# Gate and up of a SwiGLU layer: Strassen's seven products in every second step, sums on VectorE

## The chip, the core and the metric

The kernel runs on one core of one Trainium2 chip. The metric is the device time of one execution in microseconds. A core has TensorE for matrix products, VectorE, ScalarE and GpSimd for the rest, an SBUF of 128 partitions and a PSUM of eight banks (128 x 512 float32 each). Every engine has a queue of its own instructions and goes through it in order; SP here only issues transfers.

## The reference

One decoder layer for 256 tokens of width 2048 in float32. Two token mixers (an attention with compressed, selected and windowed keys, and a gated delta rule) work on the same normalised input, are merged by gates, projected and added to x. What the change touches is the feed-forward part behind them, with D_FF = 5632:

```python
x = x + mix @ w_out
h2 = _rms_norm(x, ffn_norm)
x = x + (jax.nn.silu(h2 @ w_gate) * (h2 @ w_up)) @ w_down
```

All weights and activations are float32.

## The kernel before

The 256 tokens are two tiles of 128 (t = 0, 1), the width of 2048 is 16 k-tiles of 128, and D_FF is 11 blocks of 512 columns. A weight tile of two k-tiles by 512 columns is loaded as `raw` [128, 2, 512] (512 KB) by SP, in `load_pair` (L99). Products are made in a reduced float32 format; to keep the precision, each operand is split into a high part (the number in that format) and a low part (the rest), and a product takes three matmuls: high by high, high by low, low by high. ScalarE copies raw to `whi` (L107), VectorE subtracts to `wlo` (L108):

```python
hi = stream.tile([P, 2, 512], F32R, tag="whi", name=nm("whi"), bufs=3)
lo = stream.tile([P, 2, 512], F32R, tag="wlo", name=nm("wlo"), bufs=3)
nc.scalar.activation(hi[:, :, :width], raw[:, :, :width], AF.Copy)
nc.vector.tensor_tensor(
    lo[:, :, :width], raw[:, :, :width], hi[:, :, :width].bitcast(F32), ALU.subtract
```

`raw` has four buffers, `whi` and `wlo` three each, all in the pool `stream`. A tile of raw is free again when its two readers, the copy and the subtraction, are done.

`chunk_tok` (L113) multiplies the activations (stationary, one k-tile by 128 tokens at a time) with 512 columns of weights, for both tiles of tokens, into two PSUM banks. For each pair of k-tiles it issues 12 matmuls of 128 x 128 by 128 x 512 (L122 to L124: two k-tiles, two token tiles, three each). For gate and up it runs over 8 pairs, so 96 matmuls, and a block of gate and up has 192.

A block of gate and up is one `chunk_tok` for w_gate, whose `evac_gate` (L1051) writes Silu(PSUM x rs2) on ScalarE into `sg` (rs2 is the reciprocal norm of each token), and one for w_up, whose `evac_up` (L1058) multiplies with PSUM and rs2 on VectorE; then `transpose_hilo` (L179) turns the result in eight transposes on TensorE (L183) and splits it (L176 on ScalarE, L177 on VectorE) into the tiles `act` in SBUF, the stationary operand of w_down. Eleven blocks follow each other, then four chunks of 512 columns of w_down over all 44 k-tiles, whose result is added to x2 (L1078) and written out.

The program is written in the order of the loops, and a scheduler that comes with the language puts the instructions of each engine into their final order by its own model of their times. So an engine's queue need not follow the code line by line; the excerpts of the order below show what came out.

Of the kernel before, what the change touches and what calls it, by code (L numbers as in the profile page):

```python
# [1115 lines left out]
```

## Time and profile before

| | us |
|---|---|
| median of three runs | 1974.73 (1974.52 to 1977.64) |
| span of the profiled execution | 1971.1 |
| TensorE busy in it | 1946.4 |
| VectorE busy | 1155.0 |
| ScalarE busy | 928.4 |
| from the transposes of one gate/up block to those of the next | 44.41 |

The time of a run is the device's, the span that of the profiled execution from its first to its last instruction. Busy times are summed over an engine's instructions; a busy TensorE counts matmuls that lie in its pipeline, so 1946.4 of 1971.1 says that it hardly ever stood, not that it ran at its peak. The last row is read from the chain that ended last.

### The profile page before, as it was taken

What the parts mean: (1) busy time and instruction counts of PE and PEld (TensorE: products, weight loads), DVE (VectorE), ACT (ScalarE), POOL (GpSimd) and SP (SyncE); (2) the same over time, 40 slices, a digit from 0 to 9 for tenths busy, and PEclk for the clock granted to TensorE, in tenths of its full rate; (3) what the DMA queues carried; (4) which work ended last, traced back from release to release, by engine and by line L of the source; (5) the groups of instructions that cost most, each with busy time, mean ns of one, the idle gap of its engine ahead of it and who ended that gap; (6) DMA issues with size and microseconds to landing.
All of it is one profiled execution on the core that took longest, in us unless ns stands there. A gap on an engine that the chain in (4) does not pass through costs nothing.

```text
span 1971.1 us, 27260 instructions
## 1 busy us (share of the span) xinstructions
PE 1946.4 (99%) x10485; PEld 1651.0 (84%) x10485; DVE 1155.0 (59%) x1715; ACT 928.4 (47%) x1377; POOL 54.1 (3%) x97
## 2 busy tenths in 40 slices
PE   8999999999999999999999999999999999999999
PEld 6878877876998998999987788888888888888887
DVE  5555766655468587687774665554455444544443
ACT  5434555555454554654543544444444444443333
POOL 0001000001000000100100000000000000000000
PEclk9999999999999999999999999999999999999999
DMA  8566545546767566566574965666666666656663
GB/s 231 170 183 193 161 129 162 170 149 200 217 173 203 169 178 198 158 193 166 153 200 157 333 201 183 191 192 183 191 191 186 191 191 191 191 185 201 201 202 130
DMA packets 207605, 367.04 MB, mean 186 GB/s; under 512 B 25473, under 2 KB 34546, under 8 KB 207090
## 3 DMA queue, kind: packets, MB, share of 16 engines
q1 hardware_dynamic: 207442, 365.28, 62.1%
q8 instruction: 82, 1.34, 0.3%
q14 instruction: 49, 0.40, 0.1%
q10 hardware_dynamic: 32, 0.01, 0.0%
HBM read 355.76 MB, written 9.45 MB: 185 GB/s over the span
## 4 chain that ended last, share of the span: by engine, by line
PE 96%; DMA 2%; DVE 1%; ACT 0%; SPq 0%; issue 0%; POOL 0%; ACTq 0%; POOLq 0%; DVEq 0%
PE mm L123 25%; PE mm L124 24%; PE mm L122 24%; PE mm L141 4%; PE mm L143 4%; PE mm L142 4%; PE sd L183 1%; PE sd L668 1%; PE sd L448 1%; PE sd L561 1%; DMA Q<-grow_d 1%; PE sd L748 1%; DMA raw<-in_w_branch_b_dram 1%; PE sd L567 1%; PE sd L568 0%; PE sd L267 0%
## 5 line engine op out<-in xcount | busy, mean ns | idle before, releaser
L108 DVE TENSOR_TENSOR wlo<-raw,whi 128x1024 fp32r<-128x1024 f32 x632 | 773.7, 1225 | 658.5 <-ACT whi L107 656.1
L107 ACT ACTIVATE whi<-raw 128x1024 fp32r<-128x1024 f32 x632 | 669.7, 1060 | 804.5 <-PE mm L124 674.4
L123 PE MATMUL mm<-wlo,hT_hi 128*128 128x512 f32 x704 | 276.7, 393 | 0.0
L124 PE MATMUL mm<-whi,hT_lo 128*128 128x512 f32 x704 | 276.5, 393 | 0.0
L124 PE MATMUL mm<-whi,h2T_lo 128*128 128x512 f32 x704 | 274.0, 389 | 0.0
L123 PE MATMUL mm<-wlo,h2T_hi 128*128 128x512 f32 x704 | 273.9, 389 | 0.0
L122 PE MATMUL mm<-whi,hT_hi 128*128 128x512 f32 x704 | 260.2, 393 | 0.0
L122 PE MATMUL mm<-whi,h2T_hi 128*128 128x512 f32 x704 | 249.9, 390 | 0.0
L143 PE MATMUL mm<-hT_hi,wlo 128*128 128x256 f32 x768 | 218.4, 285 | 0.0
L141 PE MATMUL mm<-hT_hi,whi 128*128 128x256 f32 x768 | 218.4, 285 | 0.0
L142 PE MATMUL mm<-hT_lo,whi 128*128 128x256 f32 x768 | 218.3, 284 | 0.0
L124 PEld LDWEIGHTS mm<-whi,hT_lo 128*128 128x128 f32 x704 | 132.3, 188 | 27.7 <-issue 1.1
L123 PEld LDWEIGHTS mm<-wlo,hT_hi 128*128 128x128 f32 x704 | 132.3, 188 | 27.5 <-issue 1.1
L124 PEld LDWEIGHTS mm<-whi,h2T_lo 128*128 128x128 f32 x704 | 132.2, 188 | 27.5
L122 PEld LDWEIGHTS mm<-whi,h2T_hi 128*128 128x128 f32 x704 | 132.2, 188 | 27.1
L123 PEld LDWEIGHTS mm<-wlo,h2T_hi 128*128 128x128 f32 x704 | 132.2, 188 | 27.0
L122 PEld LDWEIGHTS mm<-whi,hT_hi 128*128 128x128 f32 x704 | 132.1, 188 | 26.3 <-issue 0.2
L141 PEld LDWEIGHTS mm<-hT_hi,whi 128*128 128x128 f32 x768 | 147.2, 192 | 0.6
L142 PEld LDWEIGHTS mm<-hT_lo,whi 128*128 128x128 f32 x768 | 147.2, 192 | 0.2
L143 PEld LDWEIGHTS mm<-hT_hi,wlo 128*128 128x128 f32 x768 | 146.9, 192 | 0.4
L123 PE MATMUL mm<-wlo,act 128*128 128x512 f32 x352 | 138.5, 393 | 0.0
L124 PE MATMUL mm<-whi,act 128*128 128x512 f32 x352 | 138.4, 393 | 0.0
...
## 6 DMA issues: line engine op xcount, KB each, us to landing
raw<-in_w_in_dram SPq DMA_DIRECT2D x272, 512.0 KB, 3.7
raw<-in_w_gate_dram SPq DMA_DIRECT2D x88, 512.0 KB, 4.4
raw<-in_w_up_dram SPq DMA_DIRECT2D x88, 512.0 KB, 3.7
raw<-in_w_down_dram SPq DMA_DIRECT2D x88, 512.0 KB, 4.7
raw<-in_w_branch_a_dram SPq DMA_DIRECT2D x32, 512.0 KB, 4.7
raw<-in_w_branch_b_dram SPq DMA_DIRECT2D x32, 512.0 KB, 4.9
raw<-in_w_out_dram SPq DMA_DIRECT2D x32, 512.0 KB, 4.7
...
```

Source lines behind the costliest of these rows:

```text
L107: nc.scalar.activation(hi[:, :, :width], raw[:, :, :width], AF.Copy)
L108: nc.vector.tensor_tensor(lo[:, :, :width], raw[:, :, :width], hi[:, :, :width].bitcast(F32), ALU.subtract)
L122: nc.tensor.matmul(o, lhsT=sh, rhs=hi[:, j, :width], start=kt == 0, stop=False)
L123: nc.tensor.matmul(o, lhsT=sh, rhs=lo[:, j, :width], start=False, stop=False)
L124: nc.tensor.matmul(o, lhsT=sl, rhs=hi[:, j, :width], start=False, stop=kt == kts - 1)
L141: nc.tensor.matmul(o, lhsT=hi[:, j, ws], rhs=xh[:, kt, :], start=first, stop=False, skip_group_check=True)
L142: nc.tensor.matmul(o, lhsT=hi[:, j, ws], rhs=xl[:, kt, :], start=False, stop=False, skip_group_check=True)
L143: nc.tensor.matmul(o, lhsT=lo[:, j, ws], rhs=xh[:, kt, :], start=False, stop=last, skip_group_check=True)
L183: nc.tensor.transpose(pt[:, i * P : (i + 1) * P], s4, ident)
L448: nc.tensor.matmul(pc[:60, :P], lhsT=kp[:, l0 + l, :], rhs=wc[:, l, :], start=l0 + l == 0, stop=l0 + l == 31)
L561: nc.tensor.transpose(pt[:n, r * P : (r + 1) * P], pb[:, r, c0 : c0 + n], ident)
L567: nc.tensor.matmul(po, lhsT=wh, rhs=ph[:n], start=i == 0, stop=False)
```

## The change

Eleven blocks become one as before (block 0) and ten new ones. Block 0 writes its result to DRAM (`act_d`) in place of transposing it. Beside its matmuls, a side task `factors` makes the stationary operands of the new blocks: it multiplies the normalised activations by the token's norm (a row of norms, `rsrow`, comes from one matmul with ones), takes the sums that Strassen's scheme needs, and splits them, 13 tiles `Fh` and `Fl` for each of four groups of k-tiles.

In the new blocks gate and up are multiplied together. Step j (0 to 7) takes k-tiles j and 8 + j of w_gate and of w_up, so four tiles of 128 x 512, in two raw tiles of 512 KB (`raw_step`). The two k-tiles, the two token tiles, and gate and up make a product of 2 x 2 blocks by 2 x 2 blocks. An odd step (`eight_step`) takes its eight products, 24 matmuls. An even step (`seven_step`) takes seven, 21 matmuls, of which four have sums of weight tiles as their moving operand. These sums are made on VectorE, four of 128 x 512 for a step (tiles `ta` and `tb`), and then split into `thi` on ScalarE and `tlo` on VectorE like the weights; of the tile of up only one half is split. The products go to seven PSUM banks `M`, in which the eight products of the odd steps are accumulated too, so that gate and up come out by the same few sums. These are taken once at the end of a block: one copy, two Silu on ScalarE and nine operations on VectorE (`strassen_block`). Blocks 1 and 2 transpose and split their result into SBUF at once (`act_r`). Blocks 3 to 10 write theirs to `act_d`. The first chunk of w_down begins with blocks 1 and 2; beside it a side task `act_in` brings the other nine blocks back from DRAM, transposes and splits them.

The order on TensorE, in its matmuls until w_out has ended, is as before; the program has 9951 matmuls in place of 10070.

The order on VectorE shows what stands there in the place of the weights' subtractions. Before, in the middle of gate/up, VectorE has the subtractions of one raw tile after another, and at a block's end two multiplications and the two splits:

```order
L108 TENSOR_TENSOR wlo_2421_14740<-raw_2419_14737,whi_2420_14739 128x1024
L108 TENSOR_TENSOR wlo_2424_14758<-raw_2422_14755,whi_2423_14757 128x1024
L108 TENSOR_TENSOR wlo_2431_14794<-raw_2429_14791,whi_2430_14793 128x1024
L108 TENSOR_TENSOR wlo_2434_14812<-raw_2432_14809,whi_2433_14811 128x1024
L1058 SCALAR_TENSOR_TENSOR sg_2397_14623<-mm_2399_14627,rs2_11664,sg_2397_14623 128x512
L1058 SCALAR_TENSOR_TENSOR sg_2398_14625<-mm_2400_14628,rs2_11664,sg_2398_14625 128x512
L108 TENSOR_TENSOR wlo_2437_14830<-raw_2435_14827,whi_2436_14829 128x1024
```

Now, in block 7 at its third step (step 2: raw_2455 is its gate tile, raw_2456 its up tile; raw_2467 and raw_2468 are those of step 3, raw_2473 is the gate tile of step 4; y_2429 belongs to the end of block 6), VectorE has these twelve rows:

```order
L1157 TENSOR_TENSOR ta_2457_14343<-raw_2455_14339,raw_2456_14341 128x512
L1158 TENSOR_TENSOR ta_2457_14343<-raw_2456_14341 128x512
L182 TENSOR_TENSOR wlo_2460_14350<-raw_2455_14339,whi_2459_14349 128x1024
L1208 TENSOR_TENSOR y_2429_14234<-y_2429_14234,v_2427_14232 128x512
L1160 TENSOR_TENSOR tb_2458_14346<-ta_2457_14343,raw_2456_14341 128x512
L182 TENSOR_TENSOR tlo_2462_14354<-ta_2457_14343,thi_2461_14353 128x1024
L182 TENSOR_TENSOR wlo_2466_14362<-raw_2456_14341,whi_2465_14361 128x512
L1161 TENSOR_TENSOR tb_2458_14346<-tb_2458_14346,raw_2455_14339 128x512
L182 TENSOR_TENSOR wlo_2470_14391<-raw_2467_14386,whi_2469_14390 128x1024
L182 TENSOR_TENSOR wlo_2472_14395<-raw_2468_14388,whi_2471_14394 128x1024
L182 TENSOR_TENSOR tlo_2464_14358<-tb_2458_14346,thi_2463_14357 128x1024
L182 TENSOR_TENSOR wlo_2478_14433<-raw_2473_14422,whi_2477_14432 128x1024
```

The sums stand between the subtractions, and the last row is the first for the next step of seven. Beyond this excerpt the sums ta of step 4 follow.

In block 2 the rows stand in another order. Here raw_2033 is the up tile of step 1, raw_2038 and raw_2039 are the gate and up tiles of step 2, raw_2050 and raw_2051 those of step 3, raw_2056 and raw_2057 those of step 4:

```order
L182 TENSOR_TENSOR wlo_2037_12515<-raw_2033_12508,whi_2036_12514 128x1024
L182 TENSOR_TENSOR wlo_2043_12553<-raw_2038_12542,whi_2042_12552 128x1024
L182 TENSOR_TENSOR wlo_2049_12565<-raw_2039_12544,whi_2048_12564 128x512
L182 TENSOR_TENSOR wlo_2053_12594<-raw_2050_12589,whi_2052_12593 128x1024
L1157 TENSOR_TENSOR ta_2058_12629<-raw_2056_12625,raw_2057_12627 128x512
L1158 TENSOR_TENSOR ta_2058_12629<-raw_2057_12627 128x512
L1160 TENSOR_TENSOR tb_2059_12632<-ta_2058_12629,raw_2057_12627 128x512
L182 TENSOR_TENSOR wlo_2055_12598<-raw_2051_12591,whi_2054_12597 128x1024
```

Here the last subtractions that read the tiles of step 2 stand two and three rows ahead of the first sum of step 4.

The core of the diff; what is left out are comments, the moving of pools, and the closing of those that are no longer used:

```diff
-    def chunk_tok(w, c0, width, kts, stat, evac):
-        ps = [psm.tile([P, 512], F32, tag="mm", name=nm("mm")) for _ in range(NT)]
-        for k0 in range(0, kts, 2):
+    def chunk_tok(w, c0, width, kts, stat, evac, order=None):
+        ps = [mps() for _ in range(NT)]
+        pairs = order or list(range(0, kts, 2))
+        for n, k0 in enumerate(pairs):
             hi, lo = load_pair(w, k0, c0, width)
             for j in range(2):
-                kt = k0 + j
+                first, last = n + j == 0, j == 1 and n == len(pairs) - 1
                 for t in range(NT):
-                    sh, sl = stat(kt, t)
+                    sh, sl = stat(k0 + j, t)
                     o = ps[t][:, :width]
-                    nc.tensor.matmul(o, lhsT=sh, rhs=hi[:, j, :width], start=kt == 0, stop=False)
+                    nc.tensor.matmul(o, lhsT=sh, rhs=hi[:, j, :width], start=first, stop=False)
                     nc.tensor.matmul(o, lhsT=sh, rhs=lo[:, j, :width], start=False, stop=False)
-                    nc.tensor.matmul(o, lhsT=sl, rhs=hi[:, j, :width], start=False, stop=kt == kts - 1)
+                    nc.tensor.matmul(o, lhsT=sl, rhs=hi[:, j, :width], start=False, stop=last)
             yield
...
+    A12, A11, A22, S1, S3, S2, S4 = range(7)
+    B12, B11, B22, B21, B3, B5 = range(7, 13)
+    Fh = [fac.tile([P, 13, P], F32R, name=f"Fh{g}") for g in range(4)]
+    Fl = [fac.tile([P, 13, P], F32R, name=f"Fl{g}") for g in range(4)]
+    def tmp(n):
+        return fin.tile([P, 512], F32, tag="tmp", name=nm(n), bufs=6)
+    def factors():
+        dg = tmp("dg")
+        for t in range(NT):
+            nc.vector.tensor_scalar_mul(dg[:, t * P : (t + 1) * P], ident, rs2[:, t : t + 1])
+        one = tmp("one")
+        nc.vector.memset(one[:, :P], 1.0)
+        pr = sps()
+        nc.tensor.matmul(pr[:, :S], lhsT=one[:, :P], rhs=dg[:, :S], start=True, stop=True)
+        nc.scalar.activation(rsrow, pr[:, :S], AF.Copy)
+        yield
+        hv = h2T_hi.bitcast(F32).rearrange("p (h k) s -> p h k s", h=2)
+        lv = h2T_lo.bitcast(F32).rearrange("p (h k) s -> p h k s", h=2)
+        for g in range(4):
+            js = slice(2 * g, 2 * g + 2)
+            q = ft.tile([P, 4, 2, P], F32, tag="q", name=nm("q"))
+            for t in range(NT):
+                ts = slice(t * P, (t + 1) * P)
+                qt = q[:, 2 * t : 2 * t + 2]
+                nc.vector.tensor_tensor(qt, hv[:, :, js, ts], lv[:, :, js, ts], ALU.add)
+                qf = qt.rearrange("p h k c -> p (h k) c")
+                nc.vector.tensor_tensor(qf, qf, rsrow[:, ts].unsqueeze(1).to_broadcast([P, 4, P]), ALU.mult)
+            yield
+            sm = ft.tile([P, 6, P], F32, tag="sm", name=nm("sm"))
+            e, o = q[:, :, 0, :], q[:, :, 1, :]
+            nc.vector.tensor_tensor(sm[:, 0], e[:, 3], e[:, 2], ALU.subtract)
+            nc.vector.tensor_tensor(sm[:, 1], e[:, 1], e[:, 3], ALU.subtract)
+            nc.vector.tensor_tensor(sm[:, 2], e[:, 1], sm[:, 0], ALU.subtract)
+            nc.vector.tensor_tensor(sm[:, 3], e[:, 0], sm[:, 2], ALU.subtract)
+            nc.vector.tensor_tensor(sm[:, 4], o[:, 1], o[:, 3], ALU.subtract)
+            nc.vector.tensor_tensor(sm[:, 5], o[:, 0], o[:, 2], ALU.subtract)
+            hilo(Fh[g][:, 0:3], Fl[g][:, 0:3], e[:, 0:3])
+            hilo(Fh[g][:, 3:7], Fl[g][:, 3:7], sm[:, 0:4])
+            hilo(Fh[g][:, 7:11], Fl[g][:, 7:11], o)
+            hilo(Fh[g][:, 11:13], Fl[g][:, 11:13], sm[:, 4:6])
+            yield
...
-    def evac_gate(c):
-        def f(t, ps):
-            sg[t] = fin.tile([P, 512], F32, tag="tmp", name=nm("sg"), bufs=6)
-            nc.scalar.activation(sg[t], ps, AF.Silu, scale=rs2[:, t : t + 1])
-
-        return f
-
-    def evac_up(c):
-        def f(t, ps):
-            a = sg[t]
-            nc.vector.scalar_tensor_tensor(a, ps, rs2[:, t : t + 1], a, ALU.mult, ALU.mult)
-            k0 = 4 * c
-            transpose_hilo(
-                [a[:, i * P : (i + 1) * P] for i in range(4)], act[0][k0 // 16], act[1][k0 // 16], k0 % 16, t
-            )
-
-        return f
-
-    for c in range(DFF // 512):
-        run(chunk_tok(w_gate, c * 512, 512, KD, stat_h2, evac_gate(c)))
-        run(chunk_tok(w_up, c * 512, 512, KD, stat_h2, evac_up(c)))
+    def evac_gate(t, ps):
+        sg[t] = tmp("sg")
+        nc.scalar.activation(sg[t], ps, AF.Silu, scale=rs2[:, t : t + 1])
+    def evac_up(t, ps):
+        nc.vector.scalar_tensor_tensor(sg[t], ps, rs2[:, t : t + 1], sg[t], ALU.mult, ALU.mult)
+        nc.sync.dma_start(act_d[0, t], sg[t])
+    side.append(factors())
+    run(chunk_tok(w_gate, 0, 512, KD, stat_h2, evac_gate))
+    run(chunk_tok(w_up, 0, 512, KD, stat_h2, evac_up))
+    drain()
...
+    def split(src, n, pool, tag, bufs):
+        hi = pool.tile([P, 2, 512], F32R, tag=tag[0], name=nm(tag[0]), bufs=bufs)
+        lo = pool.tile([P, 2, 512], F32R, tag=tag[1], name=nm(tag[1]), bufs=bufs)
+        hilo(hi[:, :n], lo[:, :n], src[:, :n])
+        return hi, lo
+    def raw_step(j, c):
+        raw = []
+        for n in ("g", "u"):
+            raw.append(stream.tile([P, 2, 512], F32, tag="raw", name=nm("raw")))
+            nc.sync.dma_start(raw[-1], halves[n][j][:, :, c * 512 : (c + 1) * 512])
+        return raw
+    def products(terms, M, j, first, last):
+        seen, final = set(), {m: i for i, (m, *_) in enumerate(terms)}
+        g = j // 2
+        for i, (m, f, hi, lo) in enumerate(terms):
+            nc.tensor.matmul(M[m], lhsT=Fh[g][:, f], rhs=hi, start=first and m not in seen, stop=False)
+            nc.tensor.matmul(M[m], lhsT=Fh[g][:, f], rhs=lo, start=False, stop=False)
+            nc.tensor.matmul(M[m], lhsT=Fl[g][:, f], rhs=hi, start=False, stop=m in last and final[m] == i)
+            seen.add(m)
+    def seven_step(j, c, M):
+        g, u = raw_step(j, c)
+        b21, b11, b22, b12 = g[:, 0], g[:, 1], u[:, 0], u[:, 1]
+        ta = sw.tile([P, 2, 512], F32, tag="T", name=nm("ta"), bufs=3)
+        nc.vector.tensor_tensor(ta[:, 0], b11, b12, ALU.add)
+        nc.vector.tensor_tensor(ta[:, 1], b22, b12, ALU.add)
+        tb = sw.tile([P, 2, 512], F32, tag="T", name=nm("tb"), bufs=3)
+        nc.vector.tensor_tensor(tb[:, 0], ta[:, 0], b22, ALU.add)
+        nc.vector.tensor_tensor(tb[:, 1], tb[:, 0], b21, ALU.add)
+        gh, gl = split(g, 2, stream, ("whi", "wlo"), 3)
+        ah, al = split(ta, 2, sw, ("thi", "tlo"), 4)
+        bh, bl = split(tb, 2, sw, ("thi", "tlo"), 4)
+        uh, ul = split(u, 1, stream, ("whi", "wlo"), 3)
+        terms = [
+            (1, A11, gh[:, 1], gl[:, 1]),
+            (2, A12, gh[:, 0], gl[:, 0]),
+            (7, S3, ah[:, 1], al[:, 1]),
+            (5, S1, ah[:, 0], al[:, 0]),
+            (6, S2, bh[:, 0], bl[:, 0]),
+            (4, A22, bh[:, 1], bl[:, 1]),
+            (3, S4, uh[:, 0], ul[:, 0]),
+        ]
+        if j == 0:
+            terms = [terms[i] for i in (0, 4, 2, 3, 6, 5, 1)]
+        products(terms, M, j, j == 0, (1, 6, 7) if j == 6 else ())
+    def eight_step(j, c, M):
+        g, u = raw_step(j, c)
+        gh, gl = split(g, 2, stream, ("whi", "wlo"), 3)
+        uh, ul = split(u, 2, stream, ("whi", "wlo"), 3)
+        u0, u1, g0, g1 = ((h[:, i], l[:, i]) for h, l in ((uh, ul), (gh, gl)) for i in range(2))
+        if j == 7:
+            terms = [(5, B22, *u0), (5, B21, *u1), (3, B5, *u0), (3, B3, *u1)]
+            terms += [(4, B22, *g0), (4, B21, *g1), (2, B12, *g0), (2, B11, *g1)]
+        else:
+            terms = [(4, B22, *g0), (4, B21, *g1), (2, B12, *g0), (2, B11, *g1)]
+            terms += [(5, B22, *u0), (5, B21, *u1), (3, B5, *u0), (3, B3, *u1)]
+        products(terms, M, j, False, (2, 3, 4, 5) if j == 7 else ())
+    def strassen_block(c):
+        M = {m: mps() for m in (1, 6, 7, 5)}
+        M.update({m: sps() for m in (3, 4, 2)})
+        for j in range(8):
+            (eight_step if j % 2 else seven_step)(j, c, M)
+        m1, v, x, y = tmp("m1"), tmp("v"), tmp("x"), tmp("y")
+        nc.scalar.activation(m1, M[1], AF.Copy)
+        nc.vector.tensor_tensor(v, M[6], m1, ALU.subtract)
+        nc.vector.tensor_tensor(y, v, M[7], ALU.subtract)
+        nc.vector.tensor_tensor(x, M[5], v, ALU.add)
+        nc.vector.tensor_tensor(v, M[5], y, ALU.add)
+        nc.vector.tensor_tensor(x, M[3], x, ALU.add)
+        nc.vector.tensor_tensor(y, M[4], y, ALU.subtract)
+        nc.scalar.activation(y, y, AF.Silu)
+        nc.vector.tensor_tensor(m1, M[2], m1, ALU.add)
+        nc.scalar.activation(m1, m1, AF.Silu)
+        nc.vector.tensor_tensor(y, y, v, ALU.mult)
+        nc.vector.tensor_tensor(x, m1, x, ALU.mult)
+        for t, a in enumerate((x, y)):
+            if c > 2:
+                nc.sync.dma_start(act_d[c, t], a)
+                continue
+            pt = sps()
+            for i in range(4):
+                nc.tensor.transpose(pt[:, i * P : (i + 1) * P], a[:, i * P : (i + 1) * P], ident)
+            ks, ts = slice(4 * c - 4, 4 * c), slice(t * P, (t + 1) * P)
+            hilo(act_r[0][:, ks, ts], act_r[1][:, ks, ts], pt.rearrange("p (k c) -> p k c", k=4))
+    for c in range(1, NB):
+        strassen_block(c)
...
+    rest = [0] + list(range(3, NB))
+    act_l = {c: [actp.tile([P, 4, S], F32R, name=f"act{q}_{c}") for q in range(2)] for c in rest}
+    def act_in():
+        for c in rest:
+            for t in range(NT):
+                a = tmp("a")
+                nc.sync.dma_start(a, act_d[c, t])
+                transpose_hilo([a[:, i * P : (i + 1) * P] for i in range(4)], act_l[c][0], act_l[c][1], 0, t)
+            yield
 
     def stat_act(kt, t):
...
+    order = [4 * c + k for c in [1, 2] + rest for k in (0, 2)]
+    side.append(act_in())
     for c in range(4):
-        run(chunk_tok(w_down, c * 512, 512, KF, stat_act, evac_down(c)))
+        run(chunk_tok(w_down, c * 512, 512, KF, stat_act, evac_down(c), order), 1)
```

## Rows read from the trace of the kernel before

**Rows 1.** The page's first part: busy time, share of the span, instructions.

```profile
span 1971.1 us, 27260 instructions
PE 1946.4 (99%) x10485; PEld 1651.0 (84%) x10485; DVE 1155.0 (59%) x1715; ACT 928.4 (47%) x1377; POOL 54.1 (3%) x97
```

**Rows 2.** The page's fourth part: the chain that ended last, by engine.

```profile
PE 96%; DMA 2%; DVE 1%; ACT 0%; SPq 0%; issue 0%; POOL 0%; ACTq 0%; POOLq 0%; DVEq 0%
```

**Rows 3.** Busy time by engine in one gate/up block (windows; columns first).

```profile
core 0: us, PE busy (x) PEld busy (x) DVE busy (x) ACT busy (x) POOL busy (x), PEclk, DMA share, GB/s
1282.40:1326.80 44.40, 44.40 (x203) 36.87 (x201) 22.21 (x21) 19.32 (x20) 0.00 (x0) 1.00 0.65 191
```

**Rows 4.** The chain in order of time, gate/up: start, us, what.

```profile
1282.42 0.87 PE sd L183 x8
1326.83 0.87 PE sd L183 x8
```

**Rows 5.** TensorE's timeline in gate/up: start, us, line, operation.

```profile
1374.73 0.39 PE L122 MATMUL mm<-whi,h2T_hi 128*128 128x512 f32 x1
1374.96 0.39 PE L123 MATMUL mm<-wlo,h2T_hi 128*128 128x512 f32 x1
1375.19 0.39 PE L124 MATMUL mm<-whi,h2T_lo 128*128 128x512 f32 x1
```

**Rows 6.** VectorE by line and shape: count | busy, mean ns | idle before, releaser.

```profile
L108 DVE TENSOR_TENSOR wlo<-raw,whi 128x1024 fp32r<-128x1024 f32 x632 | 773.7, 1225 | 658.5 <-ACT whi L107 656.1
...
L708 DVE TENSOR_SCALAR Q<-Q,gcum 128x128 f32<-128x128 f32 x32 | 7.1, 281 | 6.7 <-DMA Q<-grow_d 6.7
...
L989 DVE TENSOR_TENSOR ba<-ba,ga 128x512 f32<-128x512 f32 x8 | 5.5, 682 | 2.1 <-DMA ba<-brA_d 2.1
...
L1078 DVE TENSOR_TENSOR x<-mm,x 128x512 f32<-128x512 f32 x8 | 5.2, 684 | 5.4 <-PE mm L124 5.4
```

**Rows 7.** VectorE's timeline at two places in gate/up.

```profile
1498.18 1.23 DVE L108 TENSOR_TENSOR wlo<-raw,whi 128x1024 fp32r<-128x1024 f32 x1 [1.49 <-ACT whi L107]
1499.33 1.40 DVE L1058 SCALAR_TENSOR_TENSOR sg<-mm,rs,sg 128x512 f32<-128x512 f32 x2
...
1372.37 1.29 DVE L177 TENSOR_TENSOR act<-sd,act 128x512 fp32r<-128x512 f32 x2 [0.80 <-ACT act L176]
```

**Rows 8.** ScalarE by line and shape, the split of a weight tile.

```profile
L107 ACT ACTIVATE whi<-raw 128x1024 fp32r<-128x1024 f32 x632 | 669.7, 1060 | 804.5 <-PE mm L124 674.4 <-PE mm L142 73.3 <-issue 31.1
```

**Rows 9.** Waits in gate/up, 1250 to 1720: total us, times, longest.

```profile
ACT whi L107 <- PE mm L124: 239.8, 148, 1.7
DVE wlo L108 <- ACT whi L107: 229.2, 169, 3.3
ACT act L176 <- PE sd L183: 14.2, 10, 1.4
```

**Rows 10.** The page's sixth part: transfers, KB each, median us to landing.

```profile
raw<-in_w_gate_dram SPq DMA_DIRECT2D x88, 512.0 KB, 4.4
raw<-in_w_up_dram SPq DMA_DIRECT2D x88, 512.0 KB, 3.7
```

**Rows 11.** The tile raw, 642.4 to 643.3: two loads, issue and landing.

```profile
L101 SPq DMA_DIRECT2D raw<-in_w_in_dram x2: 452/460/467, 642.6 to 643.1; - x2
...
DMA to landing us min/median/max: 3.8/4.2/4.6
```

**Rows 12.** Busy time by engine behind a long wait, as Rows 3.

```profile
1085.00:1090.00 5.00, 4.99 (x12) 3.92 (x13) 0.82 (x2) 1.06 (x1) 0.00 (x0) 0.50 0.83 272
1095.00:1102.00 7.00, 6.43 (x31) 5.24 (x31) 5.91 (x8) 2.82 (x5) 0.00 (x0) 1.00 1.02 413
```

**Rows 13.** TensorE's timeline at the wait ahead of it.

```profile
1083.08 0.30 PE L668 MATMUL sd<-ident,y 128*128 128x128 f32 x1 [3.52 <-DVE y L871]
```

More of the change, by code (lines that the diff above doesn't have):

```diff
@@ L97, in sps, with mps @@
         return pss.tile([P, 512], F32, tag="sd", name=nm("sd"))
+    def mps():
+        return psm.tile([P, 512], F32, tag="mm", name=nm("mm"))
     def load_pair(w, k0, c0, width):
@@ L130, in chunk_feat @@
     def chunk_feat(w, c0, evac, xh, xl):
-        ps = [psm.tile([P, 512], F32, tag="mm", name=nm("mm")) for _ in range(2)]
+        ps = [mps() for _ in range(2)]
         for k0 in range(0, KD, 2):
@@ L1000, in tile_hybrid_block @@
     scr.__exit__(None, None, None)
-    fin = ctx.enter_context(tc.tile_pool(name="fin", bufs=1))
-    gain2 = fin.tile([P, D], F32, name="gain2", tag="gain2")
+    fin = ctx.enter_context(tc.tile_pool(name="fin", bufs=1, side="right"))
+    x2 = fin.tile([P, NT, D], F32, name="x2")
+    gap = fin.tile([P, 72], F32, name="gap")
+    nc.gpsimd.memset(gap[:, :1], 0.0)
+    ss2 = fin.tile([P, NT, 4], F32, name="ss2")
+    rs2 = fin.tile([P, NT], F32, name="rs2")
+    sst = fin.tile([P, NT], F32, name="sst")
+    rsrow = fin.tile([P, S], F32, name="rsrow")
+    hp_cm = tc.tile_pool(name="hp", bufs=1, side="right")
+    hp = hp_cm.__enter__()
+    gain2 = hp.tile([P, D], F32, name="gain2", tag="gain2")
     nc.sync.dma_start(gain2, ffn_norm.partition_broadcast(P).rearrange("p o d -> p (o d)"))
@@ L1027, in tile_hybrid_block @@
         run(chunk_tok(w_out, c * 512, 512, KD, stat_of(mixT_hi, mixT_lo), evac_out(c)))
-    act = [[], []]
-    for q in range(2):
-        for i in range(3):
-            if i == 2:
-                act[q].append(fin.tile([P, 12, S], F32R, name=f"act{q}{i}"))
-            elif i == 1:
-                act[q].append(fin.tile([P, 16, S], F32R, name=f"act{q}{i}"))
-            else:
-                act[q].append(big_tile(f"act{q}{i}", F32R))
-    rs2 = fin.tile([P, NT], F32, name="rs2")
-    sst = fin.tile([P, NT], F32, name="sst")
+    NB = DFF // 512
+    big_cm.__exit__(None, None, None)
+    fac_cm = tc.tile_pool(name="fac", bufs=1, reuse_waits="tile")
+    fac = fac_cm.__enter__()
+    ft_cm = tc.tile_pool(name="ft", bufs=2, reuse_waits="tile")
+    ft = ft_cm.__enter__()
+    act_d = dram.tile([NB, NT, P, 512], F32, name="act_d", bufs=1)
     nc.vector.tensor_reduce(sst, ss2, AX.X, ALU.add)
@@ new lines, in tile_hybrid_block @@
+    run(chunk_tok(w_gate, 0, 512, KD, stat_h2, evac_gate))
+    run(chunk_tok(w_up, 0, 512, KD, stat_h2, evac_up))
+    drain()
+    hp_cm.__exit__(None, None, None)
+    ft_cm.__exit__(None, None, None)
+    late = ctx.enter_context(tc.tile_pool(name="late", bufs=1, side="right", reuse_waits="tile"))
+    act_r = [late.tile([P, 8, S], F32R, name=f"act_r{q}") for q in range(2)]
+    sw_cm = tc.tile_pool(name="sw", bufs=4, side="right", reuse_waits="tile")
+    sw = sw_cm.__enter__()
+    halves = {
+        "g": w_gate.rearrange("(h j p) c -> j p h c", h=2, p=P),
+        "u": w_up.rearrange("(h j p) c -> j p h c", h=2, p=P),
+    }
@@ new lines, in tile_hybrid_block @@
+    for c in range(1, NB):
+        strassen_block(c)
+    sw_cm.__exit__(None, None, None)
+    fac_cm.__exit__(None, None, None)
+    actp = ctx.enter_context(tc.tile_pool(name="actp", bufs=1, reuse_waits="tile"))
+    rest = [0] + list(range(3, NB))
[7 more added lines that the diff above has]
+            yield
```

15 lines of the change are left out of this document (8 added, 7 removed).

## The prediction

> **What bounds the kernel now.** I read the page first. Of the span of 1971.1 us TensorE is busy 1946.4, VectorE 1155.0 [rows 1], and the chain that ended last is TensorE for 96% [rows 2]. The median of the runs is 1974.73, 3.6 above the profiled span; I add every change to the median.
>
> Then the stretch that is changed. In the chain in order of time, the transposes that close a gate/up block stand at 1282.42 and 1326.83 [rows 4]: a block takes 44.41 us, of which 0.87 are transposes; 43.54 us are left for 192 matmuls, 0.2268 us each, which is the distance of their starts in the timeline [rows 5]. In that block TensorE is busy 44.40 of 44.40 us, VectorE 22.21, ScalarE 19.32, the DMA 0.65 [rows 3]. VectorE and ScalarE wait for TensorE and for each other [rows 9]: the tiles of weights are made ahead of their use, and nothing but TensorE sets the pace.
>
> **What the change removes.** A step of seven does 21 matmuls in place of 24. Four such steps in each of ten blocks remove 120 matmuls: 120 x 0.2268 = 27.2 us. A new block has 180 of them, 40.8 us. The order of instructions holds them gone, so this part is certain; it is what TensorE would save if it never waited. The transposes stay as many.
>
> **What it adds on VectorE.** Rows in the timeline that follow each other without a wait give the distance of starts: 1498.18 to 1499.33, 1.14 to 1.15 us for 128x1024; two of 128x512 in 1.29 us of which the last takes 0.69, so 0.60 [rows 7]. It is the same from PSUM and from SBUF: 0.684 and 0.682 us each [rows 6]. A steady block has, for four pairs of steps, 16 sums, 4 short and 12 + 8 long subtractions, and 9 operations at the end: 29 x 0.602 + 20 x 1.14 = 40.3 us. VectorE goes from half busy to as much work as TensorE has (40.8). Operations beside TensorE cost nothing only while one of the two is idle half the time; that cover is gone.
>
> **What the sums wait for.** This term decides. The tiles raw have four slots. In the new order two serve the steps of seven and two those of eight, always the same, so the loads of a step of seven cannot begin before the last reader of the step of seven before it. A gate load lands 4.4 us after issue (4.45 used), one of up 3.7 [rows 10]. Of two issued 0.5 us apart the first landed after 3.8, the second after 4.6, so 1.3 behind it [rows 11]; at the highest rate seen, 413 GB/s, 512 KB take 1.27 us [rows 12]. A step of seven issues gate and up 0.6 us apart. Up alone would land 0.6 + 3.7 = 4.3 after gate's issue, queued behind gate 4.45 + 1.27 = 5.7: these are the bounds, and I take about the middle, 5.1. A split on ScalarE takes 1.06 us [rows 8].
>
> Down the new VectorE rows of block 7 (the excerpt of the order above that begins with ta_2457), from the first ta of step 2 on: wlo of up ends at 5.4, its slot takes the gate load of step 4, landed at 9.85, split by 10.95. VectorE would start wlo_2478 at 9.3: it waits 1.7. From the last reader in step 4 to ta of step 6 lie 0.6 + 4 x 1.14 = 5.2 us of work against 4.3 to 5.7 for the load: 0 to 0.6, taken as 0. From there to ta of the next block 0.6 + 3 x 1.14 and a wait of 0.6 for thi, whose source tb ends only two rows ahead: 4.6 us after the gate slot is free, against 4.3 to 5.7: 0.5. The y that needs ScalarE waits some 0.4. Together 3.2 (2.7 to 4.8): a steady block takes 43.5 us, as long as the 43.54 before.
>
> In blocks 1 to 3 the order is worse: the last readers of both raw tiles stand two or three rows ahead of the ta that needs the next ones (second excerpt above: 0.6 + 1.14 us of work against 5.1). In the same way I get waits of 1.8, 3.5, 2.7 and 2.7 in block 1, 3.5 and 1.6 more in block 2, 3.5, 1.6 and 1.6 in block 3.
>
> Sum, from the end of block 0 on TensorE to the first end operation of each block: block 1: 34.5 us of VectorE rows + 11.9 of waits (the four, and 1.2 for a thi) = 46.4; blocks 2 and 3: 40.3 + 1.2 (two more lo of the kept activations) + 6.5 = 48 each; block 4: 42; blocks 5 to 10: 6 x 43.5 = 261. That is 445.4; TensorE ends 2.3 later (ten matmuls behind the last wlo), 447.7, against 10 x 43.54 = 435.4 before: +12.3 us.
>
> **The two ends.** Factors, beside block 0: on VectorE 16 wide operations, 24 of 128 columns (at most 0.28, as L708 [rows 6]) and 16 subtractions of at most 0.60: up to 26 us, with 16 x 1.14 for the weights and the evacuation 45.6 against 43.5 on TensorE: 0 to 4 us late, I take 2, and 1.2 for the last subtractions ahead of the evacuation. One 128x256 matmul more is 0.1. At w_down 18 tiles of 256 KB come back from DRAM in front of the loads. Blocks 1 and 2 stay in SBUF and give TensorE 4 x 2.8 us; the first tile from DRAM is loaded long before, the later ones share SP's queue with the raw loads: 0 to 4, taken as 1.5. Writing them is hidden (512 KB in a block of 8.4 MB).
>
> Sum: 12.3 + 3.3 + 1.5 = +17: **1992 us**, by itself 1984 (short queueing) to 2010 (long queueing, both ends dear).
>
> The Trainium skill, DMA: Bandwidth & Descriptors, Anatomy of one DMA, gives a transfer 2.0 us and its bytes at 436 GB/s, which is an estimate of 3.2 us for 512 KB; it is fitted on another issue path. By it the waits nearly go, and the sum would be about 1976. The rows say 3.7 and 4.4 [rows 10], and they decide.
>
> **Rivals.**
> A, *the loads are hidden.* If the raw tiles always lie ready (in the block before, ScalarE waits for TensorE, never for a raw load [rows 9]), VectorE's 40.3 us, the waits for thi and y and TensorE's 40.8 make blocks of about 41.2: 36 + 42.3 + 41.5 + 7 x 41.2 = 408 + 2.3, less 435.4, and the ends at 4.8: -20, **1955 us**. It decides once a gate load with its split takes under about 4 us from the slot's release. For it: the rows of before load one tile in 2.72 us, the mean rate is the same. Against: there a slot is loaded four steps ahead, here one.
> B, *landing as short as up's.* Both loads land after 3.7 without queueing: the first wait shrinks to 0.9, the others go; steady blocks 42.1, blocks 1 to 3 by 1 to 2 less: **1979 us**, hardly to be told from no change.
> C, *the clock.* Before, one wait of TensorE of 3.52 us [rows 13] is followed by a stretch at a granted clock of 0.50, 1.2 GHz, with 12 matmuls in 5 us in place of 22 [rows 12]. The waits of blocks 1 to 3 and the start of block 1, where TensorE has 11 matmuls for some 8 us of VectorE, are as long. Each such stretch costs TensorE some 3 us, of which the 7 us that it has over in these blocks hide part: up to 14 more, **2006 us**. The Trainium skill, TensorE: Matmul & The Clock Gate, HAM oscillation, describes a kernel that lost its clock this way at every wait for a DMA; the trace agrees in the one place named.
> That the matmuls are not removed can't be: the order shows it.
>
> **Chances.** The forecast 0.55, A 0.23, B 0.12, C 0.10. Three runs spread by 0.16%, so 0.2% is about what a measurement can tell: 4 us, 1970.8 to 1978.7. Faster: A and a little else, 0.24. Same: most of B, 0.09. Slower: 0.67. The range reaches from A, 1956, to 2010.
>
> **What would show it.** In the waits view VectorE's ta and ScalarE's whi should wait for loads of w_gate and w_up, some 30 us over ten blocks, ta longest in blocks 1 to 3 (about 3 us); VectorE should be over 0.9 busy in the stretch, TensorE about 0.93 with waits for wlo and tlo; blocks 5 to 10 should take 43 to 45 us, 2 and 3 near 48. Landings under 4 us or issues far ahead of need would make me wrong towards A; blocks of 41 us show it at once. A landing beyond 5 us, or a granted clock under 0.95 there, would push it up.

## The result and the profile after

The changed kernel takes 1993.59 us in the median of four runs (1990.94 to 1995.01) against 1974.89 before: 1.0097 times as long, interval 1.0084 to 1.0109. 1992 had been forecast. The page of its profiled execution (1995.01 us by its time, the slowest of the four) shows the new balance of the engines: its span and first part, and from its fourth part the first row of the chain that ended last.

```profile
span 1993.3 us, 27527 instructions
PE 1938.4 (97%) x10367; PEld 1636.7 (82%) x10367; DVE 1374.5 (69%) x2084; ACT 998.2 (50%) x1484; POOL 54.3 (3%) x98
PE 82%; DVE 9%; DMA 6%; issue 1%; ACT 1%; SPq 0%; POOL 0%; DVEq 0%; ACTq 0%; POOLq 0%
```

TensorE is busy hardly less than in [rows 1], although 119 matmuls are gone, and its share of the chain has fallen from 96% [rows 2] to 82%: VectorE and loads stand there now. The same kind of row as [rows 3], from one block's first end operation (v on VectorE, L1199) to the next: blocks 2, 3, 4, 7 and 8, and a stretch at the start of block 3.

```profile
core 0: us, PE busy (x) PEld busy (x) DVE busy (x) ACT busy (x) POOL busy (x), PEclk, DMA share, GB/s
1331.53:1384.27 52.74, 46.27 (x183) 36.76 (x184) 43.41 (x53) 25.56 (x29) 0.00 (x0) 0.90 0.53 159
1384.27:1436.26 51.99, 48.13 (x194) 37.88 (x193) 42.62 (x54) 27.36 (x31) 0.00 (x0) 0.90 0.51 162
1436.26:1478.36 42.10, 40.08 (x176) 32.54 (x175) 39.98 (x49) 22.99 (x26) 0.00 (x0) 1.00 0.67 211
1566.91:1609.58 42.67, 40.76 (x179) 33.10 (x178) 40.59 (x51) 24.64 (x27) 0.00 (x0) 1.00 0.62 208
1609.58:1651.95 42.37, 41.10 (x181) 33.38 (x179) 40.58 (x50) 24.63 (x27) 0.00 (x0) 1.00 0.63 210
1392.42:1402.66 10.24, 9.27 (x24) 6.40 (x25) 10.15 (x15) 4.78 (x6) 0.00 (x0) 0.50 0.30 113
```

In a late block both engines are full: VectorE busy 40.6 of 42.4 us, TensorE 41.1. In blocks 2 and 3 neither is: they take ten microseconds more, VectorE stands for nine microseconds of each, and the granted clock is 0.90. From the waits of the whole stretch (1283 to 1742), as [rows 9]:

```profile
ACT whi L181 <- PE sd L1150: 79.6, 61, 3.9
...
DVE wlo L182 <- ACT whi L181: 20.8, 16, 3.6
DVE ta L1157 <- DMA raw<-in_w_up_dram: 20.4, 17, 3.7
ACT whi L181 <- DMA raw<-in_w_gate_dram: 14.9, 16, 2.5
...
PE mm L1148 <- ACT thi L181: 12.9, 10, 2.5
```

There are the waits that were forecast, of ta for the load of up (20.4) and of a split for the load of gate (14.9). Behind them stands one that was not: VectorE 20.8 us for whi, which ScalarE makes late because TensorE still holds the three tiles of whi. The loads that answer to [rows 10]:

```profile
raw<-in_w_gate_dram SPq DMA_DIRECT2D x88, 512.0 KB, 3.8
raw<-in_w_up_dram SPq DMA_DIRECT2D x88, 512.0 KB, 4.5
```

Up is now the later one, 4.5 behind its own issue, which in a step of seven is 0.6 behind gate's: 5.1, as was taken. The estimate of 3.2 us for 512 KB worked out from the Trainium skill (DMA: Bandwidth & Descriptors, Anatomy of one DMA) is not reached here either.

**Phases.** From the starts of matmuls in the two traces, and what the prediction's terms give for the same phases (the transposes counted where they now stand):

| phase | before, us | after, us | moved | forecast |
|---|---|---|---|---|
| to the first matmul of gate/up | 1233.1 | 1236.8 | +3.7 | 0 |
| block 0, first to last matmul | 44.2 | 46.2 | +2.0 | +3.3 |
| ten blocks | 444.5 | 458.7 | +14.2 | +5.3 |
| w_down to the end | 249.4 | 251.6 | +2.2 | +8.5 |

The first is no part of the change: in the experiments that keep the changed kernel's program up to there, this matmul starts between 1233.2 and 1236.1, and in e8 and e12, which keep the program of the kernel before, at 1235.5 and 1235.6. In the other three, one term was too small and one too large.

### The profile page after: what moved, and what is told of

Its sections match the earlier page's. It is cut to its first block, busy times and chain, and to the rows that moved or that the text cites. A ratio compares the mean times of both kernels' runs of the same rounds, so it can differ in the third digit from the quotient of the medians.

```text
span 1993.3 us, 27527 instructions
## 1 busy us (share of the span) xinstructions
PE 1938.4 (97%) x10367; PEld 1636.7 (82%) x10367; DVE 1374.5 (69%) x2084; ACT 998.2 (50%) x1484; POOL 54.3 (3%) x98
## 4 chain that ended last, share of the span: by engine, by line
PE 82%; DVE 9%; DMA 6%; issue 1%; ACT 1%; SPq 0%; POOL 0%; DVEq 0%; ACTq 0%; POOLq 0%
PE mm L128 17%; PE mm L129 17%; PE mm L127 16%; PE mm L146 4%; PE mm L148 4%; PE mm L147 4%; DMA raw<-in_w_up_dram 3%; DVE wlo L182 3%; PE sd L1148 2%; PE sd L1149 2%; PE sd L1150 2%; DVE tlo L182 2%; PE mm L1148 1%; PE mm L1149 1%; PE mm L1150 1%
## 5 line engine op out<-in xcount | busy, mean ns | idle before, releaser
L112 DVE TENSOR_TENSOR wlo<-raw,whi 128x1024 fp32r<-128x1024 f32 x472 | 577.7, 1226 | 415.7 <-ACT whi L111 413.5
L111 ACT ACTIVATE whi<-raw 128x1024 fp32r<-128x1024 f32 x472 | 500.2, 1061 | 565.7 <-PE mm L129 430.1
L181 ACT ACTIVATE whi<-raw 128x1024 fp32r<-128x1024 f32 (+1 forms) x160 | 151.1, 949 | 114.9 <-PE sd L1150 79.6
L182 DVE TENSOR_TENSOR wlo<-raw,whi 128x1024 fp32r<-128x1024 f32 (+1 forms) x160 | 172.7, 1087 | 21.6 <-ACT whi L181 20.8
L1149 PE MATMUL sd<-wlo,Fh 128*128 128x512 f32 x320 | 126.9, 397 | 7.1 <-DVE wlo L182 7.0
L1148 PE MATMUL sd<-whi,Fh 128*128 128x512 f32 x320 | 125.0, 397 | 1.1 <-ACT whi L181 1.1
L1150 PE MATMUL sd<-whi,Fl 128*128 128x512 f32 x320 | 126.1, 394 | 0.0
L128 PE MATMUL mm<-wlo,act 128*128 128x512 f32 x288 | 112.4, 390 | 0.0
L129 PE MATMUL mm<-whi,act 128*128 128x512 f32 x288 | 112.2, 389 | 0.0
L127 PE MATMUL mm<-whi,act 128*128 128x512 f32 x288 | 102.0, 389 | 0.0
```

The lines of the kernel that those rows point to most:

```text
L112: nc.vector.tensor_tensor(lo[:, :, :width], raw[:, :, :width], hi[:, :, :width].bitcast(F32), ALU.subtract)
L127: nc.tensor.matmul(o, lhsT=sh, rhs=hi[:, j, :width], start=first, stop=False)
L182: nc.vector.tensor_tensor(dst_lo, src, dst_hi.bitcast(F32), ALU.subtract)
L1148: nc.tensor.matmul(M[m], lhsT=Fh[g][:, f], rhs=hi, start=first and m not in seen, stop=False)
L1149: nc.tensor.matmul(M[m], lhsT=Fh[g][:, f], rhs=lo, start=False, stop=False)
L1150: nc.tensor.matmul(M[m], lhsT=Fl[g][:, f], rhs=hi, start=False, stop=m in last and final[m] == i)
```

## The experiments

The table has all of them. The two columns of blocks are distances between starts of the same end operation (v; in e4 the first Silu): for the changed kernel these three rows of VectorE's timeline, for blocks 1, 3 and 10:

```profile
1331.53 0.68 DVE L1199 TENSOR_TENSOR v<-mm,m 128x512 f32<-128x512 f32 x1
...
1436.26 0.68 DVE L1199 TENSOR_TENSOR v<-mm,m 128x512 f32<-128x512 f32 x1
...
1736.05 0.69 DVE L1199 TENSOR_TENSOR v<-mm,m 128x512 f32<-128x512 f32 x1 [0.28 <-PE mm L1150]
```

| kernel | us | to before (interval) | blocks 2, 3 | blocks 4 to 10 |
|---|---|---|---|---|
| forecast | 1992 | | 96 | 303 |
| changed | 1993.59 | 1.0097 (1.0084 to 1.0109) | 104.7 | 299.8 |
| e1 ring | 2004.29 | 1.0159 (1.0143 to 1.0174) | 107.0 | 309.7 |
| e2 no sums | 1988.72 | 1.0085 (1.0068 to 1.0103) | 101.3 | 314.3 |
| e3 two sevens | 1973.15 | 1.0000 (0.9991 to 1.0009) | 93.3 | 296.1 |
| e4 no seven | 1970.36 | 0.9985 (0.9975 to 0.9994) | 89.0 | 304.6 |
| e5 ring, sums held back | 1980.89 | 1.0031 (1.0020 to 1.0042) | 94.3 | 297.5 |
| e6 sums held back | 1977.19 | 1.0019 (1.0010 to 1.0029) | 96.7 | 295.8 |
| e7 tiles for half of up | 1975.29 | 1.0008 (0.9999 to 1.0017) | 98.3 | 293.8 |
| e8 before, 32 bytes on | 1974.08 | 1.0001 (0.9992 to 1.0011) | | |
| e9 none kept | 1981.08 | 1.0038 (1.0023 to 1.0053) | 87.8 | 298.3 |
| e10 e9 with e7 | 1967.85 | 0.9966 (0.9952 to 0.9980) | 84.2 | 298.2 |
| e11 e10, three sevens | 1974.14 | 1.0000 (0.9990 to 1.0009) | 86.3 | 294.0 |
| e12 before, act lower | 1969.22 | 0.9978 (0.9969 to 0.9988) | | |

TensorE's matmuls alone would be 285.8 us for seven blocks of 180, 295.3 of 186, 304.8 of 192.

**e1.** Four slots more, for the steps of seven alone:

```diff
-            raw.append(stream.tile([P, 2, 512], F32, tag="raw", name=nm("raw")))
+            if seven:
+                raw.append(sw.tile([P, 2, 512], F32, tag="raws", name=nm("raws"), bufs=4))
+            else:
+                raw.append(stream.tile([P, 2, 512], F32, tag="raw", name=nm("raw")))
```

> Only the number of buffers changes: the raw tiles of the steps of seven get four slots of their own beside the four of raw, so a load can begin one whole step of seven earlier. Theory (late loads on a full VectorE): the waits of ta and of whi for w_gate and w_up go, blocks 1 to 10 fall from 458 us in all to about 420 (VectorE 40.3 us of rows and about 1 of waits for a block), the granted clock stays at 1.00 because TensorE has no long waits left, time about 1955 us. Rival (VectorE is simply full, the loads are a symptom): blocks stay at 42 to 44 and the time within 1980 to 1994.

Slower still, and both theories miss. The waits:

```profile
DVE ta L1160 <- DMA raws<-in_w_up_dram: 37.4, 28, 2.5
```

One of them in VectorE's timeline:

```profile
1521.59 0.69 DVE L1160 TENSOR_TENSOR ta<-raws,raws 128x512 f32<-128x512 f32 x1 [2.33 <-DMA raws<-in_w_up_dram]
```

ta waits longer with twice the slots. In the order of this kernel the planner has moved ta further ahead, from block 2 on to 1.1 to 4.7 us of VectorE rows behind the row that frees its slot. VectorE takes its rows in turn, so a wait at ta also holds up the subtractions behind it. More slots by themselves are no cure.

**e2.** The sums left out:

```diff
-        ta = sw.tile([P, 2, 512], F32, tag="T", name=nm("ta"), bufs=3)
...
-        nc.vector.tensor_tensor(tb[:, 1], tb[:, 0], b21, ALU.add)
+        ta, tb = g, u
```

> The four sums of a step of seven are left out, the splits of ta and tb read the raw tiles instead (the products are then of the weights alone, not of their sums). VectorE has 9.6 us less in a block, the four slots stay. Theory: a wait for a load costs only what VectorE has no room for; with 10 us of room in a block they are hidden, blocks of 41 to 42 us, time 1955 to 1965 us. Rival (the loads alone set the pace, whatever VectorE has to do): blocks of 43 us and more, time over 1980 us.

The theory falls, the rival holds: 314.3 us for blocks 4 to 10, 44.9 each. The wait has gone to ScalarE, which takes its splits in turn as well:

```profile
ACT thi L181 <- DMA raw<-in_w_gate_dram: 105.9, 33, 6.2
```

So late loads need no full VectorE to cost time; an engine that has to read a raw tile before it has landed, with other work behind it in its queue, is enough.

**e3 and e4.** Fewer steps of seven. The factors of an even step by eight are its own pieces and two differences:

```diff
-            (eight_step if j % 2 else seven_step)(j, c, M)
+            (seven_step if j in SEVEN else eight_step)(j, c, M)
...
+            if 2 * g not in SEVEN:
+                nc.vector.tensor_tensor(sm[:, 0], e[:, 1], e[:, 3], ALU.subtract)
+                nc.vector.tensor_tensor(sm[:, 1], e[:, 0], e[:, 2], ALU.subtract)
...
+                hilo(Fh[g][:, 0:4], Fl[g][:, 0:4], e)
+                hilo(Fh[g][:, 4:6], Fl[g][:, 4:6], sm[:, 0:2])
```

> Two steps of seven in a block (0 and 4), the other six by eight. 186 matmuls are 42.2 us of TensorE in a block, VectorE has 19 rows of 0.602 and 18 of 1.14, 32.0 us. Theory: VectorE has room again, the blocks take 42.2 to 42.7 us, time about 1961 us: half of the removed matmuls bring more than all of them. Rival (the block's structure itself, with its loads in pairs and its end, costs time): over 1975 us.

> No step of seven: all eight steps of a block by eight products, the block's end two multiplications and one sum, everything else of the change kept (factors, results by way of DRAM, the order of w_down). 192 matmuls, 43.5 us in a block. Theory: the rest of the change costs hardly anything, 1973 us (1970 to 1977), as before the change. Rival (the rest of the change costs what was lost): about 1990 us.

e4 is as the theory had it: 43.5 us a block, and what the change has besides the steps of seven costs little: e4 is 3 us faster than before, where the quicker matmuls of w_down that e12 explains are worth 4.5. The steps of seven as they stand in the changed kernel lose 23.2 us to it (1993.59 to 1970.36) with 27.2 us less to do. In e3 blocks 4 to 10 are at TensorE's pace, 296.1 against 295.3, as forecast; but blocks 2 and 3 take 93.3 against 84.4 for their matmuls, and the time misses its 1961.

**e5 and e6.** The planner is kept from moving ta ahead: one element of it is first written from the subtraction of the eight-step before (e5 with e1's slots, e6 without).

```diff
         ta = sw.tile([P, 2, 512], F32, tag="T", name=nm("ta"), bufs=3)
+        if held:
+            nc.gpsimd.tensor_copy(ta[:, 0, :1], held[-1])
...
+        held.append(ul[:, 0, :1].bitcast(F32))
```

> The ring run overturned the simple theory: with eight slots ta still waits 37 us, because the planner then puts ta still earlier on VectorE, 1.1 to 3.5 us of rows behind the row that frees its slot. New theory (order): what counts is how much VectorE work stands between the last reader of a slot and the sum that reads the next load in it; it has to be more than the 5.1 us of a load. This kernel has the four slots of e1 and holds ta back: one element of ta is first written from the wlo of the eight-step before, so the planner cannot place the sum ahead of that subtraction. The order then has 5.2 us of rows or more everywhere. By the theory the waits for w_up and w_gate nearly go, blocks of 41 to 42 us, 1955 to 1965 us. Rival 1 (VectorE is full, the order is no matter): blocks of 43 to 45, 1985 to 2005 us. Rival 2 (the clock, lowered by waits at the blocks' starts, is the price): waits of TensorE at the starts and half clock remain, over 1975.

> The same hold, with the four slots of the changed kernel. The rows between a slot's last reader and ta are then 2.9 to 6.4 us, mostly 3.4 to 4.6, and the blocks 1 to 3 no longer have the worst of them (1.1). By the theory of the order some 20 us of waits go, mostly in blocks 1 to 3: 1970 to 1985 us. Rival (the slots alone): as the changed kernel, 1990 to 1996.

e6 lands where the theory of the order put it; e5 misses its 1955 to 1965, and shows what is left without late loads. In it the only waits for a load of gate or up are these, 7.8 us, all in block 1:

```profile
ACT whi L181 <- DMA raws<-in_w_gate_dram: 4.1, 1, 4.1
ACT whi L181 <- DMA raws<-in_w_up_dram: 2.4, 1, 2.4
DVE ta L1164 <- DMA raws<-in_w_up_dram: 1.1, 1, 1.1
DVE ta L1165 <- DMA raws<-in_w_up_dram: 0.2, 1, 0.2
```

The median falls by 12.7 us. Between the two profiled runs it is 16.6: 10.4 in blocks 2 and 3, 2.4 in block 1, 2.3 in the seven behind them. A block with its loads early takes 42.5, not 41.2 (blocks 2 and 5):

```profile
1326.35:1372.51 46.16, 43.80 (x188) 35.20 (x187) 42.52 (x51) 25.69 (x30) 0.60 (x4) 0.96 0.56 182
...
1463.70:1506.17 42.47, 41.93 (x181) 33.57 (x181) 40.78 (x50) 24.60 (x28) 1.61 (x4) 1.00 0.65 211
```

So VectorE's own rows make up most of that pace, with 40.8 of 42.5 us busy (some of it the tails of rows that overlap). Of the rest it waits 1.0 for whi and 0.7 for GpSimd, which is the hold's own price. Rival 2 has this for it: over blocks 2 and 3 (94.3) the granted clock is 0.95. Whether that is what they cost isn't shown.

**e7.** The half of up gets tiles of its own:

```diff
-        uh, ul = split(u, 1, stream, ("whi", "wlo"), 3)
+        uh = sw.tile([P, 1, 512], F32R, tag="uhi", name=nm("uhi"), bufs=3)
+        ul = sw.tile([P, 1, 512], F32R, tag="ulo", name=nm("ulo"), bufs=3)
+        hilo(uh, ul, u[:, :1])
```

> The half of the up tile that is split in a step of seven gets tiles of its own (three each of 128 x 512), so that whi and wlo have three slots for three tiles of a pair of steps in place of four. Rival theory (a raw tile is held until its split finds a free whi, so whi is the short ring): raw tiles come free earlier, 1965 to 1980 us. Theory of the order: the planner uses the room to put ta earlier again (2.3 to 4.1 us behind the slot's release, 5.8 at most), so nothing is won, 1988 to 2002 us.

The rival was right about the time, 18 us less, and my theory of the order alone was not enough. In blocks 4 to 10 the sums stand as early as before: 3.4 to 5.8 us of rows behind the last one on VectorE that reads a tile of the step of seven before, 2.3 to 6.4 in the changed kernel. There 6.0 us are won, so the shortage of whi is a second cause. In blocks 1 to 3 the planner has put most sums later than in the changed kernel (all but one 3.4 us of rows or more behind that row, where five stood at 1.1), so the 9.7 us won there can't be given to either cause alone.

**e9 and e10.** No block's result is transposed during gate/up. e10 has the tiles of e7 as well.

```diff
-            if c > 2:
-                nc.sync.dma_start(act_d[c, t], a)
-                continue
-            pt = sps()
...
+            nc.sync.dma_start(act_d[c, t], a)
...
```

> Blocks 1 and 2 write their results to DRAM like all others; nothing is transposed during gate/up, and w_down begins with blocks 0 and 1, read back. In the changed kernel blocks 2 and 3 take 52.7 and 52.0 us against 42 to 44 for the later ones, and the kept transposes stand in TensorE's queue there and wait for the sums at the end of the block before. If they are the reason, blocks 2 and 3 fall to 43 to 44, some 17 us less, 1974 to 1980 us with 2 us back at the start of w_down. If the early blocks are long only because the loads are late there (sums 1.1 us of rows behind the release of their slot), 1988 us and more.

> The same with the tiles of e7 for the half of up. If the two causes are separate, their gains add: blocks of 42 from the second on, TensorE's matmuls from the first of block 1 to the last of block 10 in 423 to 428 us (460.8 in the changed kernel, 441.0 in e7), 1959 to 1966 us. If they are one and the same wait, 1972 to 1976.

Blocks 2 and 3 fall from 104.7 to 87.8 us: the kept blocks were the reason, and the total misses its range by 1 us. How they work in the changed kernel is seen where their transposes stand. First TensorE's timeline, then ScalarE's, then VectorE's:

```profile
1342.14 0.50 PE L1148 MATMUL mm<-thi,Fh 128*128 128x512 f32 x1 [1.00 <-DVE v L1202]
...
1345.03 0.79 PE L1148 MATMUL mm<-thi,Fh 128*128 128x512 f32 x1 [1.91 <-ACT thi L181]
1345.62 1.05 PE L1216 MATMUL sd<-ident,x 128*128 128x128 f32 x4
...
1346.71 0.60 ACT L181 ACTIVATE act_r<-sd 128x512 fp32r<-128x512 f32 x1 [1.22 <-PE sd L1216]
...
1353.67 1.06 ACT L181 ACTIVATE whi<-raw 128x1024 fp32r<-128x1024 f32 x1 [2.29 <-PE sd L1150]
...
1359.12 1.06 ACT L181 ACTIVATE whi<-raw 128x1024 fp32r<-128x1024 f32 x1 [3.40 <-PE sd L1150]
...
1360.21 1.23 DVE L182 TENSOR_TENSOR wlo<-raw,whi 128x1024 fp32r<-128x1024 f32 x1 [3.62 <-ACT whi L181]
```

TensorE waits, then has four transposes in 1.05 us at half clock, ScalarE stands for them and then for whi that TensorE gives back late, and at the end VectorE, which can't make up a pause, stands for 3.62. e10, with both causes gone, is faster than before; its blocks from 2 on run at a granted clock of 1.00. Block 2:

```profile
1327.91:1371.40 43.49, 43.41 (x191) 35.50 (x190) 41.20 (x50) 23.38 (x27) 0.00 (x0) 1.00 0.64 207
```

It is 13.2 us under e9 and 7.4 under e7: the gains add in part, and 1959 to 1966 was missed by 2.

**e11.** Three steps of seven:

```diff
-    SEVEN = (0, 4)
+    SEVEN = (0, 4, 6)
```

(against e3; the rest as in e10)

> As e10 with three steps of seven (0, 4, 6) in a block. 183 matmuls are 41.5 us, VectorE has 24 rows of 0.602 and 19 of 1.14, 36.1 us. If VectorE has to have room for the waits, blocks of 41.6 to 42 us, 1954 to 1963 us, faster than e10. If e10 is at TensorE's pace already, 1962 to 1970, slower than e10 by the 30 matmuls more, 6.8 us.

Neither. Blocks 4 to 10 take 294.0 us, 4.2 less than in e10, but 3.5 of that is the last block, and behind its v the rest of the kernel takes 7.5 more. Blocks 4 to 9 take 42.7 each as against 42.8, where 183 matmuls are 41.5. So VectorE has room here and TensorE still doesn't set the pace: ta waits 35.1 us for up in 28 places in the whole stretch.

**e8 and e12, w_down.** Why w_down came out 6.3 us better than forecast is seen in TensorE's timeline of the kernel before, as [rows 5], but in w_down:

```profile
1839.22 0.40 PE L122 MATMUL mm<-whi,act 128*128 128x512 f32 x1
1839.45 0.40 PE L123 MATMUL mm<-wlo,act 128*128 128x512 f32 x1
1839.68 0.40 PE L124 MATMUL mm<-whi,act 128*128 128x512 f32 x1
1839.91 0.40 PE L123 MATMUL mm<-wlo,act 128*128 128x512 f32 x1
```

The starts are 0.23 apart to the eye; over a stretch it is 12 matmuls in 2.80 us with the tiles act of blocks 4 to 10, in place of 2.72. The change puts these tiles elsewhere, and beyond the transposes of its first chunk its matmuls are all at 0.227. e8 moves them by 32 bytes, e12 below x2:

```diff
+    gap = fin.tile([P, 8], F32, name="gap")
...
+    act_f = {(q, i): fin.tile([P, 16 if i == 1 else 12, S], F32R, name=f"act{q}{i}") for i in (1, 2) for q in range(2)}
     x2 = fin.tile([P, NT, D], F32, name="x2")
...
```

> The kernel before, with one more tile of 32 bytes a partition behind x2 (eight floats, one written by GpSimd), so that the tiles act of blocks 4 to 10 start 32 bytes later. In the kernel before, matmuls of w_down with these stand 0.233 us apart, all others, and all of the changed kernel, 0.227. If the place of the tile in SBUF is the reason, w_down loses 14 pairs of k-tiles x 12 x 0.0066 x 4 = 4.4 us: 1969 to 1971 us. If it is not, 1973 to 1975.

> The kernel before with x2 and the four tiles act in the other order in SBUF: act01 begins at 153184 (169600 before), act11 at 169568 (198272), act02 at 185952, act12 at 198240 (214656). If matmuls at 0.233 us apart come from stationary tiles that lie above some 199 kB in a partition, those of act01 and act11 go to 0.227, 8 of the 14 slow pairs of k-tiles, 2.5 us in all: 1971 to 1972 us. If not, 1973 to 1975, and the cause stays open.

e8 changes nothing. e12 gains 4.9 us, more than was said. A stretch of its w_down, and one of the kernel before with as many instructions of TensorE:

```profile
1790.00:1850.00 60.00, 60.00 (x266) 49.71 (x265) 28.33 (x25) 23.34 (x22) 0.00 (x0) 1.00 0.64 203
```

```profile
1747.30:1808.30 61.00, 61.00 (x266) 49.61 (x265) 28.16 (x24) 23.33 (x22) 0.00 (x0) 1.00 0.64 197
```

There are 266 instructions of TensorE in 60.00 us in place of 61.00, and from its first matmul to the end w_down takes 244.9 us in place of 249.4. The tiles' place is the cause (x2 moves with them, but in w_down TensorE doesn't read it). The line I had drawn at 199 kB is not: act12 still lies above it, and is quick.

## Why the prediction was right

**The time was right, and so was the main mechanism. That the total came within 2 us is luck:** the ten blocks were 8.9 us too cheap and w_down 6.3 too dear. By its own steps:

The removed matmuls and VectorE's rows were sized right: 40.3 us a block forecast, 40.6 busy in a late one. That VectorE's work takes away the cover is borne out by e3, where VectorE has room and TensorE sets the pace. Room alone isn't enough, though: in e2 and e11 VectorE has it as well, and their blocks stay at 44.9 and 42.7 us, with ScalarE or VectorE waiting in its queue for loads.

The steady blocks came out near (299.8 against 303), for another reason than the working gave. It made 41.2 us of work and 2.3 of late loads. In blocks 4 to 10 VectorE waits 5.1 us for loads, 6.5 for whi and 4.2 for thi, which is 0.7, 0.9 and 0.6 a block; some of the waits for whi come from gate's load, for which ScalarE waits 14.3. With the loads early (e5) a block is 42.5, 0.3 less, and its hold costs VectorE 0.3 a block in waits for GpSimd. So the loads cost less than the 2.3 that were taken, 0.3 to 1.7 a block. Rival A, at 41.2 with hidden loads, had its price too low, and e5 is slower than before even so.

Blocks 1 to 3 were the mis-sized term: 48.5, 52.7 and 52.0 us (from the last matmul of block 0 to the first v) against 46.4, 48 and 48. In block 1 VectorE waits 10.2 us for loads where 10.7 had been taken:

```profile
DVE ta L1157 <- DMA raw<-in_w_up_dram: 10.2, 4, 3.7
```

In blocks 2 and 3 it waits 5.1 us for loads where 11.8 had been taken (3.5 and 1.6 in block 2, 3.5, 1.6 and 1.6 in block 3), and 12.4 us for whi, which had no price there. These two waits in the changed kernel (1331.53 to 1436.26), and below them the same in e9 (1329.12 to 1416.92):

```profile
DVE wlo L182 <- ACT whi L181: 12.4, 7, 3.6
DVE ta L1157 <- DMA raw<-in_w_up_dram: 5.1, 5, 2.1
```

```profile
DVE ta L1157 <- DMA raw<-in_w_up_dram: 3.1, 4, 2.2
DVE wlo L182 <- ACT whi L181: 0.5, 1, 0.5
```

The step that failed is "40.3 + 1.2 (two more lo of the kept activations)": it priced the kept blocks by their VectorE rows alone. Their transposes and copies also stand in TensorE's and ScalarE's queues, and with the three tiles of whi that made VectorE wait. Without kept blocks (e9) the two blocks take 16.9 us less: VectorE waits 11.9 less for whi, has 3.6 less of work (82.4 us busy in place of 86.0) and waits 2.0 less for loads. The end, 2.3 us from the last v to the last matmul, took 5.7.

The clock, rival C, came true in part: 0.50, that is 1.2 GHz, in five stretches of the blocks, 30.7 us in all, each behind waits of TensorE of 1.0 to 2.6 us. The last row of the blocks' windows above is one, with 24 records in 10.24 us in place of 45; ahead of it stands in TensorE's timeline:

```profile
1390.77 0.74 PE L1148 MATMUL mm<-thi,Fh 128*128 128x512 f32 x2 [2.45 <-ACT thi L181]
```
The Trainium skill, TensorE: Matmul & The Clock Gate, HAM oscillation, describes a clock that falls at waits of TensorE, there for DMA; the trace agrees in kind, with these waits for ScalarE and VectorE. What it cost apart from the waits isn't settled; no run held the clock and kept the waits.

w_down was 6.3 us too dear: about 4.5 are the place of act (e12), which the working left out because it did not compare the starts of matmuls there with those of gate/up.
